# The last 512 output columns of a decoder block: gate folded into the weights, residual seeded into PSUM, result copied out in two halves

## The chip, the cores and the metric

The kernel runs on one NeuronCore of a Trainium2 chip. The metric is the device time of one execution in microseconds (us). The kernel before was timed three times: 1174.56, 1174.75 and 1174.26 us, median 1174.56 us. One further execution was recorded by the hardware profiler; it took 1173.49 us, and 1171.6 us of that lie between its first and its last instruction (its span). All rows of the profile below come from that one execution.

Engines are named as in the profile: PE is TensorE (matmuls; PEld are its weight loads), DVE is VectorE, ACT is ScalarE, POOL is GpSimd, SP is SyncE, which here only issues DMAs.

## What is computed

One decoder block on 256 tokens (t) of 2048 columns, everything in float32:

```
mod = silu(c) @ w_ada + b_ada;  sh1, sc1, g1, sh2, sc2, g2 = split(mod, 6)
h    = rms_norm(x) * (1 + sc1) + sh1
q, k, v, gb, gc, xt = split(h @ w_in, 6)                 # w_in 2048 x 6144
mixed = [rms_norm(attention(q, k, v)), rms_norm(gb * conv(gc * xt))]
x    = x + g1 * (mixed @ w_out)                          # w_out 2048 x 2048
h2   = rms_norm(x) * (1 + sc2) + sh2
u    = conv(h2 @ w_ffn_up)                               # w_ffn_up 2048 x 11264
ffn  = (silu(u_gate) * u_up) @ w_ffn_down                # w_ffn_down 5632 x 2048
out  = x + g2 * ffn
```

The change is about the last line. The 2048 columns of out are four groups of 512, called f = 0 to 3; g2 is one number per column.

## The kernel before

**Products.** Each float32 weight tile ("raw", 128 rows x 1024 columns: two blocks of 512) is split on the chip: ACT writes a rounded copy "hi" (line 947), and DVE or POOL writes "lo" = raw - hi (line 958). The activations are split alike. A product is three matmuls into one PSUM bank: a\*hi, a\*lo and b\*hi (lines 1194 to 1196, a and b being the two parts of the activations), or in the up projection a wide one and a narrow one (lines 1545 and 1549).

**Slots.** All weights, w_in, w_out, w_ffn_up and w_ffn_down, form one list of 205 slots of at most four blocks. While PE multiplies slot i, the program of that step lets ACT, DVE and POOL split slot i+2. SP issues all weight loads in the list's order; a load goes out when one of ten raw buffers comes free, which is when a lo is done. There are six hi and six lo buffers, so a hi waits for PE to be through with an older slot. Which step a piece of side work stands in, whether it goes ahead of or behind the splits, and whether a slot's lo's are made by POOL (table 'pool') is a dictionary of numbers, CFG, written out by hand; an engine executes its instructions in that order.

**The FFN.** The 22 groups of up columns come in four segments of 8, 5, 5 and 4; behind each segment stand the down slots for its rows of w_ffn_down. Sums of the first three segments are kept in SBUF (da). For the last one, `gate_down(f)` (lines 1518 to 1523, two token tiles of 128 each) makes x = x + g2 \* da, with g2 of the 512 columns spread over the partitions in the tile gB. So x then holds the residual and three quarters of the FFN, already gated. The last segment's down slots are 193 to 204, in the order f = 0, 1, 0, 1, 0, 1, 2, 3, 2, 3, 2, 3, with 3, 3 and 2 blocks each. So f = 3 has the slots 200, 202 and 204, and 204 is the last of the kernel; its products are ordered by token tile, all of t = 0 first.

**The end.** When f's last slot is multiplied, `evac_down` does this for each of the two token tiles:

```
y = p * gB                                               # line 1513, DVE, 128x512
y = y + x1                                               # line 1514, DVE, 128x512
out rows <- y                                            # line 1515, DMA of 256 KB, issued by SP
```

Of the kernel before, what the change touches and what calls it, by code (L numbers as in the profile page):

```python
# [234 lines left out]
               108: 3,  # L235
               109: 4,
               159: 2,
               171: 3},
# [56 lines left out]
                72: 0,  # L295
                83: 0},
       'pool_h': [4, 5, 6, 7, 8, 9, 10, 11, 15],
       'psum': [[0, 45]],
# [169 lines left out]
                 'evac_in q1 False': 2,  # L468
                 'evac_in q1 True': 3,
                 'evac_in v0 False': 2,  # L470
# [189 lines left out]
                'up_conv 0': (-1, 0.5),  # L660
                'up_conv 1': (-1, 0.5),
                'up_conv 14': (0, -1),
                'up_conv 15': (0, -0.5),
# [74 lines left out]
       'evac': [5, 0, 1],  # L738
       'sq': [3, 6, 0],
       'tr': [4, 7, 1],  # L740
       'part': -1,
       'up': [[1, 3], [1, 3], [0, 0], [2, 2]],
       'gate': [-21, -14, -2, -11],
       'cls': {'add': 2,
# [34 lines left out]
               'qk_root': 0,  # L779
               'evac_out': 1},  # L780
       'la': 2,
       'h_act': True,
       'h_lag': 1,
       'hi_late': [1, 2, 3, 5, 7, 8, 9, 10, 13, 14, 15, 17, 19, 20, 21, 25, 26, 27, 32, 33, 34, 40, 49, 50, 51, 52, 55, 56,
# [3 lines left out]


@with_exitstack  # L790
def tile_block(
# [74 lines left out]
    nc.vector.memset(ones, 1.0)  # L866
    c32 = const.tile([P, P], F32, name="c32")
    nc.vector.memset(c32, 1.0 / 32.0)
    mask = const.tile([P, 384], F32, name="mask")
    nc.gpsimd.memset(mask, 0.0)  # L870
# [70 lines left out]

    def split_hi(nb):
        ts, his = [], []
        for i in range((nb + 1) // 2):
            m = min(2, nb - 2 * i) * 512
            t = take()
            act(piece(his, "hi")[:, :m], t[:, :m], AF.Copy)  # L947
            ts.append((t, m))
        halfway.append((ts, his))
# [36 lines left out]
    class Ada:  # L986


        def __init__(self, part, c0, n, pe, psum=False):
            self.part, self.c0, self.n, self.pe, self.psum = part, c0, n, pe, psum or pe  # L990
            self.rows = 2048 // n
            self.tiles = NK // self.rows
            self.nch = n // P
            self.w = min(n, 512 if self.psum else n)
            self.seen = 0
            self.out = False
            self.own = [] if [part, c0] in CFG["own"] else None

        def want(self, r):
# [12 lines left out]
        def start(self):  # L1012
# [4 lines left out]
            else:  # L1017
                self.acc = [(t4k if self.n > 512 else t2k)(what)[:, :self.n]]

        def consume(self, r, part=None):  # L1020
            if r == 0 and part != 1:
# [4 lines left out]
            for j in range(self.rows) if part is None else range(8 * part, 8 * part + 8):  # L1026
                i = self.rows * r + j
                x = j * self.n % size
                if x == 0:
                    h = take() if self.own is None else self.own.pop(0)  # L1030
                t, last = h[:, x:x + self.n], self.own is None and x + self.n == 1024
# [45 lines left out]
        def cols(self):  # L1077
# [3 lines left out]
            for a in range(0, self.nch, 4):  # L1081
                m = min(4, self.nch - a)
                p = bank(f"adac{self.part}_{self.c0}", full=False)
                if self.nch == 1:
                    mm(p[:, 0:1], self.chunk(0), ones[:, 0:1], start=True, stop=True)
                    z = p[:, 0:1]
                else:
                    for k in range(m):
                        nc.tensor.transpose(p[:, k * P:(k + 1) * P], self.chunk(a + k), ident)
                    z = bank(f"adaz{self.part}_{self.c0}")[:, :m]  # L1090
                    V.tensor_reduce(out=z, in_=p[:, :m * P].rearrange("p (k q) -> p k q", q=P), axis=AX.X, op=ALU.add)
                self.finish(z, self.c0 + a, m, scale)

        def finish(self, z, c0, m, scale):
# [405 lines left out]
    def evac_down(seg, f):  # L1500
# [31 lines left out]
    for seg, (ga, gb_) in enumerate(SEGS):  # L1532
# [200 lines left out]
    def att_s(h):  # L1733
# [5 lines left out]
        s = t2k("s")[:, :384]  # L1739
        V.tensor_tensor(out=s, in0=p[:, :384], in1=mask, op=ALU.add)  # L1740
        m, z = small(2, "m"), small(2, "z")
        V.reduce_max(out=m[:, 0:1], in_=s[:, :128], axis=AX.X)
        V.reduce_max(out=m[:, 1:2], in_=s[:, 128:], axis=AX.X)
        i, j = (col("q", t, h) for t in range(2))
# [191 lines left out]
    for t in range(2):  # L1936
        xr.append([sb.tile([P, 1024], F32, tag="lo" if t else "hi", bufs=N_HL, name="xr") for _ in range(2)])
        for i in range(2):
            nc.sync.dma_start(xr[t][i], x[0, t * P:(t + 1) * P, i * 1024:(i + 1) * 1024])
    vb, nb = rows("vb", [(by_p(norm1_g[0]), 16), (by_p(b_ada[0]), 96)], nc.sync)  # L1940
    for _ in range(N_RAW):
# [53 lines left out]
    def slot(i):  # L1995
        more = i + LA < len(slots)
        hi_late = i == N_OUT or i in CFG["hi_late"]
        if more and not hi_late:
            split_hi(slots[i + LA][1])
        now[0] = i  # L2000
# [5 lines left out]
        if more and hi_late:  # L2006
            split_hi(slots[i + LA][1])
        steps_of(CFG["pre"].get(i, 1))
# [7 lines left out]
        if i > 1:  # L2016
            slots[i][2](*splits.pop(0))
        for g, r in extra.get(i, []):
            g.consume(r)

# [106 lines left out]
```

## Time and profile before

| | |
|---|---|
| runs of the kernel before | 1174.56, 1174.75, 1174.26 us; median 1174.56 |
| profiled execution | 1173.49 us, its span 1171.6 us |
| PE busy | 1155.4 us (99% of the span), 5989 matmuls |
| DVE, ACT, POOL busy | 917.6 (78%), 646.9 (55%), 169.3 (14%) us |
| POOL's lo's (line 958) | 61, mean 2489 ns; the same shape on DVE 1248 ns |
| clock of TensorE | 0.998 of full speed |
| HBM traffic | 320 MB, 272 GB/s over the span |

How to read it: times in a timeline are us from the span's start. A bracket behind an instruction is how long its engine had idled ahead of it and what ended the idle time. Consecutive like instructions can be put together in one row ("x4"); then the duration is from the first one's start to the last one's end. Neighbouring rows of one engine may overlap by some hundredths, since an engine is pipelined. m('D', 3, 2)0 in the names is the PSUM bank of segment 3, column group f = 2, token tile 0.

### The profile page before, as it was taken

What the parts mean: (1) busy time and instruction counts of PE and PEld (TensorE: products, weight loads), DVE (VectorE), ACT (ScalarE), POOL (GpSimd) and SP (SyncE); (2) the same over time, 40 slices, a digit from 0 to 9 for tenths busy, and PEclk for the clock granted to TensorE, in tenths of its full rate; (3) what the DMA queues carried; (4) which work ended last, traced back from release to release, by engine and by line L of the source; (5) the groups of instructions that cost most, each with busy time, mean ns of one, the idle gap of its engine ahead of it and who ended that gap; (6) DMA issues with size and microseconds to landing.
All of it is one profiled execution on the core that took longest, in us unless ns stands there. A gap on an engine that the chain in (4) does not pass through costs nothing.

```text
span 1171.6 us, 17108 instructions
## 1 busy us (share of the span) xinstructions
PE 1155.4 (99%) x5989; PEld 965.8 (82%) x5989; DVE 917.6 (78%) x1311; ACT 646.9 (55%) x1002; POOL 169.3 (14%) x100
## 2 busy tenths in 40 slices
PE   7999999999999999999999999999999999999998
PEld 5678888878777878888888888888888888888886
DVE  4469979997788989999999544768888897666785
ACT  4666565578566455556676444555435554445461
POOL 0768673631001021000000000000000000000000
PEclk9999999999999999999999999999999999999999
DMA  9999999995799989986465755576887877875541
GB/s 349 405 405 374 406 353 386 390 388 170 262 368 315 362 272 360 378 276 208 156 207 187 235 180 181 175 230 220 284 299 262 306 245 231 292 246 174 169 155 72
DMA packets 205382, 320.22 MB, mean 273 GB/s; under 512 B 13816, under 2 KB 112300, under 8 KB 205296
## 3 DMA queue, kind: packets, MB, share of 16 engines
q1 hardware_dynamic: 202336, 314.68, 77.2%
q10 hardware_dynamic: 2352, 4.22, 1.3%
q8 instruction: 47, 0.77, 0.3%
q14 instruction: 39, 0.32, 0.1%
q0 software_dynamic: 608, 0.23, 0.1%
HBM read 314.87 MB, written 4.21 MB: 272 GB/s over the span
## 4 chain that ended last, share of the span: by engine, by line
PE 91%; DMA 5%; DVE 3%; issue 1%; ACT 0%; POOL 0%; SPq 0%; DVEq 0%; POOLq 0%; ACTq 0%
PE z L1545 27%; PE z L1549 14%; DMA raw<-in_w_in_dram 2%; DMA raw<-in_w_ada_dram 2%; PE ada L1034 1%; PE mx L1194 1%; PE mx L1196 1%; PE mx L1195 1%; PE mk L1194 1%; DVE ada L1051 1%; PE mg L1194 1%; PE mg L1196 1%; PE mc L1194 1%; PE mq L1194 1%; PE mc L1196 1%; PE mg L1195 1%
## 5 line engine op out<-in xcount | busy, mean ns | idle before, releaser
L947 ACT ACTIVATE hi<-raw 128x1024 fp32r<-128x1024 f32 (+1 forms) x401 | 401.2, 1030 | 314.2 <-PE z L1545 92.9
L958 DVE TENSOR_TENSOR lo<-raw,hi 128x1024 fp32r<-128x1024 f32 x340 | 397.6, 1208 | 95.6 <-ACT hi L947 90.3
L1545 PE MATMUL z<-h,hi 128*128 128x512 f32 x1408 | 328.9, 390 | 0.0
L1545 PEld LDWEIGHTS z<-h,hi 128*128 128x128 f32 x1408 | 261.3, 188 | 52.6 <-DVE h L1440 0.3
L1051 DVE SCALAR_TENSOR_TENSOR ada<-raw,csil,ada 128x512 f32<-128x512 f32 (+2 forms) x215 | 189.0, 892 | 5.6 <-DMA raw<-in_w_ada_dram 2.0
L958 POOL TENSOR_TENSOR lo<-raw,hi 128x1024 fp32r<-128x1024 f32 x61 | 150.5, 2489 | 269.2 <-ACT hi L947 269.2
L1549 PEld LDWEIGHTS z<-h,lo 128*128 128x128 f32 x1408 | 174.8, 192 | 3.4
L1549 PE MATMUL z<-h,lo 128*128 128x256 f32 x1408 | 176.0, 283 | 0.0
L1110 POOL MEMSET gb<- 128x512 f32 x2 | 1.1, 526 | 491.8 <-DVE uy L1484 491.8
L1461 DVE TENSOR_TENSOR ub<-z,ub 128x256 f32<-128x256 f32 x120 | 43.8, 417 | 34.5 <-ACT ub L1458 34.4
L1458 ACT ACTIVATE ub<-z 128x256 f32<-128x256 f32 x120 | 39.7, 383 | 31.1 <-PE z L1545 31.0
L1477 ACT ACTIVATE uy<-ub,vcols 128x256 f32<-128x256 f32 x88 | 45.6, 593 | 6.8 <-DMA gr<-gs 6.7
L1482 DVE SCALAR_TENSOR_TENSOR uy<-ub,vcols,uy 128x255 f32<-128x255 f32 x88 | 42.1, 479 | 5.7 <-ACT uy L1477 5.6
L1484 DVE SCALAR_TENSOR_TENSOR uy<-ub,vcols,uy 128x254 f32<-128x254 f32 x88 | 42.5, 483 | 3.1
L1493 ACT ACTIVATE gh<-uy 128x512 fp32r<-128x512 f32 x22 | 13.9, 630 | 40.6 <-DVE uy L1491 40.6
L1487 ACT ACTIVATE uy<-uy 128x512 f32<-128x512 f32 x22 | 13.9, 633 | 37.2 <-DVE uy L1484 37.2
L1034 PE MATMUL ada<-raw,crep 128*32 128x512 f32 (+1 forms) x224 | 27.1, 525 | 3.2 <-DMA raw<-in_w_ada_dram 2.7
L1494 DVE TENSOR_TENSOR gl<-uy,gh 128x512 fp32r<-128x512 f32 x22 | 15.2, 693 | 17.9 <-ACT gh L1493 17.9
L1194 PE MATMUL mk<-hi,h 128*128 128x512 f32 x64 | 25.8, 403 | 0.0
L1194 PE MATMUL mq<-hi,h 128*128 128x512 f32 x64 | 25.3, 395 | 0.4 <-ACT pa_g L1214 0.4
L1194 PE MATMUL mg<-hi,h 128*128 128x512 f32 x64 | 25.7, 401 | 0.0
L1194 PE MATMUL mx<-hi,h 128*128 128x512 f32 x64 | 25.3, 396 | 0.0
(574 smaller groups left out, 1922.8 us busy)
## 6 DMA issues: line engine op xcount, KB each, us to landing
raw<-in_w_ada_dram SPq DMA_DIRECT2D x180, 512.0 KB, 6.8
raw<-in_w_ffn_up_dram SPq DMA_DIRECT2D x352, 256.0 KB, 4.7
raw<-in_w_in_dram SPq DMA_DIRECT2D x95, 512.0 KB, 7.1
raw<-in_w_ffn_down_dram SPq DMA_DIRECT2D x76, 512.0 KB, 4.7
raw<-in_w_out_dram SPq DMA_DIRECT2D x32, 512.0 KB, 6.1
raw<-in_w_ada_dram SPq DMA_DIRECT2D x24, 256.0 KB, 6.6
raw<-in_w_ffn_down_dram SPq DMA_DIRECT2D x24, 256.0 KB, 3.8
xr<-in_x_dram SPq DMA_DIRECT2D x4, 512.0 KB, 5.4
```

Source lines behind the costliest of these rows:

```text
L947: act(piece(his, "hi")[:, :m], t[:, :m], AF.Copy)
L958: (nc.gpsimd if pool in (i + 1, 3) else V).tensor_tensor(out=piece(los, "lo")[:, :m], in0=t[:, :m], in1=hi[:, :m].bitcast(F32), op=ALU.sub ...
L1034: mm(self.acc[0][q:q + 32, :], crep[:, i, :], t, start=(r == 0 and j < 4), stop=(r == self.tiles - 1 and j >= self.rows - 4), tile_positio ...
L1051: V.scalar_tensor_tensor(out=self.acc[n], in0=v, scalar=csil[:, i:i + 1], in1=acc, op0=ALU.mult, op1=ALU.add)
L1194: mm(o, a, hi[k], start=(first and k == 0 and not seeded), stop=False, skip_group_check=True)
L1458: act(c[ft // 2][:, (ft % 2) * 256:(ft % 2) * 256 + 256], zp[grp][ft][:, 256:], AF.Copy)
L1461: V.tensor_tensor(out=d, in0=zp[grp][ft][:, :256], in1=d, op=ALU.add)
L1477: act(y, b, AF.Identity, bias=fcols[3][:, i:i + 1], scale=fcols[2][:, i:i + 1])
L1482: V.scalar_tensor_tensor(out=y[:, 1:], in0=b[:, :255], scalar=fcols[1][:, i:i + 1], in1=y[:, 1:], op0=ALU.mult, op1=ALU.add)
L1484: V.scalar_tensor_tensor(out=y[:, 2:], in0=b[:, :254], scalar=fcols[0][:, i:i + 1], in1=y[:, 2:], op0=ALU.mult, op1=ALU.add)
L1545: mm(zp[grp][ft], blk(hi, j)[:, ft * P:(ft + 1) * P], h2T[k + j], start=k + j == ks[0], stop=k + j == ks[1] - 1)
L1549: mm(zp[grp][ft][:, :256], blk(lo, j)[:, ft * P:(ft + 1) * P], h2T[k + j][:, :256], start=False, stop=False)
```

## The change

For f = 3 of the last segment three things are different, switched by a new entry `'tail': [3]`:

- the raw weights of slots 200, 202 and 204 are multiplied in place by gB on DVE before they are split (line 971 of the changed kernel): three tiles of 128x1024 and two of 128x512. So the products come out gated;
- `seed_down(3)` lets ACT copy x of the two token tiles into the two PSUM banks (now named ms), one step ahead of slot 200, and all products are added onto it;
- `evac_down` only copies out: for each token tile DVE copies the first 256 columns, ACT the last 256, and each half has a DMA of 128 KB of its own, the first issued by SP, the second by ACT.

Beside it the tables are changed. Lo's go from DVE to POOL: both of slot 153, the first of slots 187, 188 and 189, both of slot 200 (in the table 'pool', 1 is the first, 3 both). One subtraction of h goes from POOL to DVE. `gate_down` for f = 2 and 3 comes four and five steps earlier (187 for 191, 177 for 182). At the second norm one DVE step of the ada projection goes from between the two token tiles of z to behind them, ahead of n2m. Some other pieces (a transposition of constants with its copy, squares of the attention output, one residual) come one or two steps earlier or in another order within a step. A constant tile of 128x128 is 128x32. The new entries 'lag', 'sets', 'xq' and 'ttr' are empty or off, and their code makes no instruction.

```diff
+                153: 3,
+                187: 1,
+                188: 1,
+                189: 1,
+                200: 3},
-       'pool_h': [4, 5, 6, 7, 8, 9, 10, 11, 15],
+       'pool_h': [5, 6, 7, 8, 9, 10, 11, 15],
...
-                'evac_c 3 1': (0, 1),
+                'evac_c 3 1': (0, 0.5),
...
-       'gate': [-21, -14, -2, -11],
+       'gate': [-21, -14, -6, -16],
...
+       'tail': [3],
...
-    def split_hi(nb):
+    gated = {}
+
+    def split_hi(n):
+        nb = slots[n][1]
         ts, his = [], []
         for i in range((nb + 1) // 2):
             m = min(2, nb - 2 * i) * 512
             t = take()
+            if n in gated:
+                w = t[:, :m].rearrange("p (k f) -> p k f", f=512)
+                V.tensor_tensor(out=w, in0=w, in1=gB[G2, gated[n]].unsqueeze(1).to_broadcast([P, m // 512, 512]),
+                                op=ALU.mult)
             act(piece(his, "hi")[:, :m], t[:, :m], AF.Copy)
...
             p = mainp["D", seg, f][t]
-            if seg == 0:
+            if seg == len(SEGS) - 1 and f in CFG["tail"]:
+                y = t2k(f"d{f}{t}")
+                V.tensor_copy(y[:, :256], p[:, :256])
+                act(y[:, 256:], p[:, 256:], AF.Copy)
+                for eng, a in ((nc.sync, 0), (nc.scalar, 256)):
+                    eng.dma_start(out[0, t * P:(t + 1) * P, f * 512 + a:f * 512 + a + 256], y[:, a:a + 256])
+            elif seg == 0:
...
+    def seed_down(f):
+        assert f"gd{f}" in done
+        key = "D", len(SEGS) - 1, f
+        whole[key] = None
+        mainp[key] = [bank(f"ms{f}{t}", keep=True, seed=True) for t in range(2)]
+        for t in range(2):
+            act(mainp[key][t], x1[t, f], AF.Copy)
...
+            if seg == len(SEGS) - 1 and f in CFG["tail"]:
+                gated[len(slots)] = f
+                if k == ka:
+                    put(len(slots) - 1, CFG["cls_seed"], seed_down, f)
```

The instructions and waits of three places, before and after. First DVE, whose last twelve instructions ahead of the end are these in the kernel before (d is the tile that goes to the output, x the residual; a wait names the engine or DMA queue):

```order
L958 TENSOR_TENSOR lo<-raw,hi 128x1024 [waits DMAHW4_49,Activation_49]
L958 TENSOR_TENSOR lo<-raw,hi 128x512 [waits DMAHW5_49,Activation_49]
L958 TENSOR_TENSOR lo<-raw,hi 128x1024 [waits DMAHW6_49,Activation_49]
L958 TENSOR_TENSOR lo<-raw,hi 128x1024 [waits DMAHW7_49,Activation_49]
L1513 TENSOR_TENSOR d_11383<-m('D', 3, 2)0_11259,gB_2_9773 128x512 [waits PE_49]
L1514 TENSOR_TENSOR d_11383<-d_11383,x_02_10095 128x512 [waits DVE_49]
L1513 TENSOR_TENSOR d_11387<-m('D', 3, 2)1_11260,gB_2_9773 128x512 [waits PE_49]
L1514 TENSOR_TENSOR d_11387<-d_11387,x_12_10097 128x512 [waits DVE_49]
L1513 TENSOR_TENSOR d_11391<-m('D', 3, 3)0_11295,gB_2_9773 128x512 [waits PE_49]
L1514 TENSOR_TENSOR d_11391<-d_11391,x_03_10131 128x512 [waits DVE_49]
L1513 TENSOR_TENSOR d_11395<-m('D', 3, 3)1_11296,gB_2_9773 128x512 [waits PE_49]
L1514 TENSOR_TENSOR d_11395<-d_11395,x_13_10133 128x512 [waits DVE_49]
```

And these in the changed kernel:

```order
L984 TENSOR_TENSOR lo<-raw,hi 128x1024 [waits Activation_49]
L984 TENSOR_TENSOR lo<-raw,hi 128x512 [waits Activation_49]
L984 TENSOR_TENSOR lo<-raw,hi 128x1024 [waits DMAHW6_49,Activation_49]
L971 TENSOR_TENSOR raw<-raw,gB_2_9773 128x1024 [waits DMAHW7_49]
L984 TENSOR_TENSOR lo<-raw,hi 128x1024 [waits Activation_49]
L1571 TENSOR_TENSOR d_11390<-m('D', 3, 2)0_11265,gB_2_9773 128x512 [waits PE_49]
L1572 TENSOR_TENSOR d_11390<-d_11390,x_02_10095 128x512 [waits DVE_49]
L1571 TENSOR_TENSOR d_11394<-m('D', 3, 2)1_11266,gB_2_9773 128x512 [waits PE_49]
L1572 TENSOR_TENSOR d_11394<-d_11394,x_12_10097 128x512 [waits DVE_49]
L1560 COPY d_11398<-ms_11245 128x256 [waits PE_49]
L1560 COPY d_11403<-ms_11246 128x256 [waits PE_49]
```

The last four instructions of 128x512 have become two copies of 128x256, and a multiplication by gB stands between the lo of slot 203 and the lo of slot 204 (the last lo).

Second ACT. Its last rows in the kernel before, ahead of the end, are the hi's of slots 202, 203 and 204:

```order
L947 ACTIVATE hi<-raw 128x1024 [waits DMAHW4_49,DVE_49,PE_49]
L947 ACTIVATE hi<-raw 128x512 [waits DMAHW5_49,DVE_49,PE_49]
L947 ACTIVATE hi<-raw 128x1024 [waits DMAHW6_49,DVE_49,PE_49]
L947 ACTIVATE hi<-raw 128x1024 [waits DMAHW7_49,DVE_49,PE_49]
L2122 UNCONDITIONAL_BRANCH
```

In the changed kernel, from the seeds on:

```order
L1589 ACTIVATE ms_11245<-x_03_10131 128x512
L1589 ACTIVATE ms_11246<-x_13_10133 128x512
L973 ACTIVATE hi<-raw 128x1024 [waits DMAHW2_49,PE_49,Activation_49]
L973 ACTIVATE hi<-raw 128x512 [waits DMAHW3_49,PE_49,Activation_49]
L973 ACTIVATE hi<-raw 128x1024 [waits DVE_49,PE_49,Activation_49]
L973 ACTIVATE hi<-raw 128x512 [waits DVE_49,PE_49,Activation_49]
L973 ACTIVATE hi<-raw 128x1024 [waits DMAHW6_49,PE_49,Pool_49]
L973 ACTIVATE hi<-raw 128x1024 [waits DVE_49,PE_49,Pool_49]
L1561 ACTIVATE d_11398<-ms_11245 128x256 [waits DVE_49]
L1563 DMA out_dram<-d_11398 128x256 [waits Activation_49]
L1561 ACTIVATE d_11403<-ms_11246 128x256 [waits DVE_49]
L1563 DMA out_dram<-d_11403 128x256 [waits DMAHW1_49,Activation_49]
```

ACT's half of each token tile waits for DVE, not for PE, and its DMA stands behind it on ACT's own queue; the hi's of the gated slots wait for DVE's multiplication.

Third POOL, from its last MEMSET but one on, before:

```order
L1110 MEMSET gb_2622 128x512
L1112 DMA gb_2622<-in_b_ada_dram 1x16x32 x4
L958 TENSOR_TENSOR lo<-raw,hi 128x1024 x7
L1110 MEMSET gb_9752 128x512
L1112 DMA gb_9752<-in_b_ada_dram 1x16x32 x4
L2122 UNCONDITIONAL_BRANCH
```

And in the changed kernel:

```order
L1162 MEMSET gb_2622 128x512
L1164 DMA gb_2622<-in_b_ada_dram 1x16x32 x4
L984 TENSOR_TENSOR lo<-raw,hi 128x1024 x9
L1162 MEMSET gb_9752 128x512
L1164 DMA gb_9752<-in_b_ada_dram 1x16x32 x4
L984 TENSOR_TENSOR lo<-raw,hi 128x1024 x4
L984 TENSOR_TENSOR lo<-raw,hi 128x512
L2229 UNCONDITIONAL_BRANCH
```

Two lo's more stand ahead of the last MEMSET (slot 153's), and five behind it, where POOL had none (those of slots 187 to 189 and of slot 200).

More of the change, by code (lines that the diff above doesn't have):

```diff
@@ L236 @@
                109: 4,
+               148: 2,
                159: 2,
@@ L738 @@
        'evac': [5, 0, 1],
-       'sq': [3, 6, 0],
+       'sq': [3, 4, 0],
        'tr': [4, 7, 1],
@@ L779 @@
                'qk_root': 0,
-               'evac_out': 1},
+               'evac_out': 1,
+               'cols_set': -1},
        'la': 2,
@@ L784 @@
        'hi_late': [1, 2, 3, 5, 7, 8, 9, 10, 13, 14, 15, 17, 19, 20, 21, 25, 26, 27, 32, 33, 34, 40, 49, 50, 51, 52, 55, 56,
[3 rows of a table removed]
[3 rows of a table added]
+       'tail': [3],
+       'lag': {},
+       'sets': [],
+       'xq': False,
+       'ttr': False}
 @with_exitstack
@@ L866, in tile_block @@
     nc.vector.memset(ones, 1.0)
-    c32 = const.tile([P, P], F32, name="c32")
+    c32 = const.tile([P, 32], F32, name="c32")
     nc.vector.memset(c32, 1.0 / 32.0)
+    pick = {}
+    for v in (1.0, 1.0 / 32.0):
+        if CFG["sets"]:
+            pick[v] = const.tile([P, 39], F32, name=f"pick{int(1 / v)}")
+            nc.gpsimd.memset(pick[v], 0.0)
+            nc.gpsimd.memset(pick[v][:, 7:8], v)
     mask = const.tile([P, 384], F32, name="mask")
@@ L997, in __init__ @@
             self.own = [] if [part, c0] in CFG["own"] else None
+            self.held = {}
         def want(self, r):
@@ L1018, in start, with hold @@
                 self.acc = [(t4k if self.n > 512 else t2k)(what)[:, :self.n]]
+        def hold(self, r):
+            tiles = self.rows * self.n // (1024 if self.own is None else 512)
+            self.held[r] = [take() if self.own is None else self.own.pop(0) for _ in range(tiles)]
         def consume(self, r, part=None):
@@ L1029, in consume @@
                 if x == 0:
-                    h = take() if self.own is None else self.own.pop(0)
+                    src = self.held.get(r, self.own)
+                    h = take() if src is None else src.pop(0)
                 t, last = h[:, x:x + self.n], self.own is None and x + self.n == 1024
@@ L1092, in cols, with cols_set @@
                 self.finish(z, self.c0 + a, m, scale)
+        def cols_set(self):
+            groups = self.set
+            p = bank(f"adas{self.part}_{self.c0}", full=False)
+            parts = [(g, a) for g in groups for a in range(0, g.nch, 4)]
+            for n, (g, a) in enumerate(parts):
+                assert g.out
+                flush(g)
+                e = pick[1.0 / 32.0 if g.pe else 1.0][:, 7 - n:39 - n]
+                m = min(4, g.nch - a)
+                for q in range(m):
+                    mm(p[32 * q:32 * q + 32, :P], e, g.chunk(a + q), start=n == 0, stop=n == len(parts) - 1,
+                       tile_position=(0, 32 * q))
+            r = t1k("adar")[:, :P]
+            act(r, p[:, :P], AF.Copy)
+            p = bank(f"adat{self.part}_{self.c0}", full=False)
+            nc.tensor.transpose(p[:, :P], r, ident)
+            for n, (g, a) in enumerate(parts):
+                m = min(4, g.nch - a)
+                g.finish(p[:, n:n + 32 * m - 31:32], g.c0 + a, m, 1.0)
         def finish(self, z, c0, m, scale):
@@ L1598, in tile_block, with in_set @@
     ready_at = {}
+    held_until = {}
+    sets = {(part, c0): n for n, e in enumerate(CFG["sets"]) for part, c0 in e}
+    filling = {}
+    def in_set(g, s):
+        n = sets.get((g.part, g.c0))
+        if n is None:
+            return False
+        filling.setdefault(n, []).append((s, g))
+        if len(filling[n]) < len(CFG["sets"][n]):
+            return True
+        s, gs = max(s for s, _ in filling[n]), [g for _, g in filling[n]]
+        gs[0].set = gs
+        at(s + 2, gs[0].cols_set)
+        ready_at.update({(g.part, g.c0 + k): s + 2 for g in gs for k in range(g.nch)})
+        return True
     def spread_loads(g, a, span):
@@ L1604, in spread_loads @@
             extra.setdefault(s, []).append((g, r))
+            lag = CFG["lag"].get(f"{g.part} {g.c0}", 0)
+            if lag:
+                s += lag
+                held_until.setdefault(s, []).append((g, r))
         at(s + 1, g.evac)
+        if in_set(g, s):
+            return
         if g.gate():
@@ L1647, in tile_block @@
             at(a, g.evac)
+            if in_set(g, a - 1):
+                continue
             at(a + 1, g.cols)
@@ L1739, in att_s @@
         s = t2k("s")[:, :384]
-        V.tensor_tensor(out=s, in0=p[:, :384], in1=mask, op=ALU.add)
         m, z = small(2, "m"), small(2, "z")
-        V.reduce_max(out=m[:, 0:1], in_=s[:, :128], axis=AX.X)
-        V.reduce_max(out=m[:, 1:2], in_=s[:, 128:], axis=AX.X)
+        if CFG["ttr"]:
+            for t, a, b in ((0, 0, 128), (1, 128, 384)):
+                V.tensor_tensor_reduce(out=s[:, a:b], in0=p[:, a:b], in1=mask[:, a:b], scale=1.0, scalar=NEG,
+                                       op0=ALU.add, op1=ALU.max, accum_out=m[:, t:t + 1])
+        else:
+            V.tensor_tensor(out=s, in0=p[:, :384], in1=mask, op=ALU.add)
+            V.reduce_max(out=m[:, 0:1], in_=s[:, :128], axis=AX.X)
+            V.reduce_max(out=m[:, 1:2], in_=s[:, 128:], axis=AX.X)
         i, j = (col("q", t, h) for t in range(2))
@@ L1938, in tile_block @@
         for i in range(2):
-            nc.sync.dma_start(xr[t][i], x[0, t * P:(t + 1) * P, i * 1024:(i + 1) * 1024])
-    vb, nb = rows("vb", [(by_p(norm1_g[0]), 16), (by_p(b_ada[0]), 96)], nc.sync)
+            (nc.scalar if CFG["xq"] and t else nc.sync).dma_start(
+                xr[t][i], x[0, t * P:(t + 1) * P, i * 1024:(i + 1) * 1024])
+    vb, nb = rows("vb", [(by_p(norm1_g[0]), 16), (by_p(b_ada[0]), 96)], nc.gpsimd if CFG["xq"] else nc.sync)
     for _ in range(N_RAW):
@@ L1998, in slot @@
         if more and not hi_late:
-            split_hi(slots[i + LA][1])
+            split_hi(i + LA)
         now[0] = i
@@ L2006, in slot @@
         if more and hi_late:
-            split_hi(slots[i + LA][1])
+            split_hi(i + LA)
         steps_of(CFG["pre"].get(i, 1))
@@ L2018, in slot @@
         for g, r in extra.get(i, []):
+            if f"{g.part} {g.c0}" in CFG["lag"] and (g, r) not in fill:
+                g.hold(r)
+            else:
+                g.consume(r)
+        for g, r in held_until.get(i, []):
             g.consume(r)
```

9 lines of the change are left out of this document (5 added, 4 removed), and 6 rows, old and new, of tables.

## Prediction

> **What bounds the kernel now.** I read the page's busy times first, then busy time by stretches, then PE's waits, and last the chain that ends the kernel. The page and the stretches:
>
> ```profile
> PE 1155.4 (99%) x5989; PEld 965.8 (82%) x5989; DVE 917.6 (78%) x1311; ACT 646.9 (55%) x1002; POOL 169.3 (14%) x100
> 0.00:41.00 41.00, 31.65 (x212) 20.74 (x213) 18.24 (x45) 19.93 (x33) 7.67 (x12) 0.96 1.00 362
> 41.00:440.00 399.00, 396.76 (x1906) 316.04 (x1905) 330.16 (x504) 245.86 (x425) 156.15 (x83) 1.00 0.94 346
> 440.00:800.00 360.00, 360.00 (x1970) 314.15 (x1969) 284.30 (x395) 203.96 (x303) 2.98 (x1) 1.00 0.70 230
> 800.00:1162.00 362.00, 362.00 (x1886) 311.04 (x1885) 279.52 (x362) 177.18 (x242) 2.49 (x5) 1.00 0.69 231
> ```
>
> The columns after the length are the busy times of PE, PEld, DVE, ACT and POOL, then the granted clock, the share of the DMA engines and GB/s. From 440 to 1162 us PE is busy for 360.00 of 360.00 and 362.00 of 362.00 us, at full clock. Nothing that another engine does there can make the kernel faster; it can only make PE wait. From 41 to 440 us PE loses 2.2 us, and its waits name these:
>
> ```profile
> PE n2b L1414 <- DVE n2d L1412: 1.0, 1, 1.0
> PE as L1737 <- ACT kT L1730: 0.9, 1, 0.9
> PE mq L1194 <- ACT pa_g L1214: 0.4, 1, 0.4
> ```
>
> Ahead of 41 us PE loses 9.35 us while the DMA engines are at 1.00; in that stretch only the constant tile is smaller. So the change can gain at two places: in those 2.3 us of waits, and behind the last products. The end, by the chain of waits, PE's last matmul and SP:
>
> ```profile
> 1162.97 0.70 DVE d L1513
> ...
> 1167.78 0.69 DVE d L1514
> 1166.62 0.39 PE L1196 MATMUL m('D', 3, 3)1_11296<-hi,gl 128*128 128x512 f32 x1
> 1168.50 0.33 SPq L1515 DMA_DIRECT2D out_dram<-d  x1
> DMA to landing us min/median/max: 2.3/2.3/2.3
> ```
>
> The chain runs through eight DVE instructions from 1162.97 on, and one could think that halving DVE's work brings 2.7 us. It does not. PE's last matmul ends at 1166.62 + 0.39 = 1167.01, and by its timeline DVE starts on that bank at 1167.05:
>
> ```profile
> 1167.05 0.69 DVE L1513 TENSOR_TENSOR d<-m('D', 3, 3)1_11296,gB 128x512 f32<-128x512 f32 x1
> ```
>
> So DVE was ready just as the products were. Behind PE's end lie 0.04 us of hand-over, two instructions until 1168.47, 0.03 us until SP issues, 2.3 us until landing (1170.8), and 0.8 us until the span's end at 1171.6. Only the first part, 1.46 us from 1167.01 to 1168.47, can shrink.
>
> **The change part by part: the end.** The bank is now copied out in two halves. Neither a DVE copy of 128x256 out of PSUM nor an ACT copy of exactly this kind is in the trace. The nearest rows:
>
> ```profile
> L880 DVE COPY vbc<-pv_vbc x1: 268/268/268, 12.8 to 12.8; 128x112 f32<-128x112 f32 x1
> L1986 DVE COPY vcols<-pv_f x1: 586/586/586, 143.1 to 143.1; 128x418 f32<-128x418 f32 x1
> L1458 ACT ACTIVATE ub<-z 128x256 f32<-128x256 f32 x120 | 39.7, 383 | 31.1 <-PE z L1545 31.0
> L1203 ACT ACTIVATE mg<-pa_g 128x512 f32<-128x512 f32 x8 | 4.5, 585 | 0.1
> ```
>
> DVE: (586 - 268) / (418 - 112) = 1.04 ns a column, so 268 + 144 x 1.04 = 0.42 us; bounds 0.27 and 0.59. ACT: 0.38 us, a read of 128x256 out of PSUM; no less, and at most the 0.59 of twice the columns. The words of the change suggest that both run side by side. The order of instructions says otherwise: ACT's half waits for DVE, and for nothing of PE's. So they run one after the other: 1167.05 + 0.42 = 1167.47 for DVE, 0.04 of hand-over (as from PE to DVE), 0.38 on ACT, end at 1167.89. ACT issues its DMA 0.03 later, at 1167.92, where SP issued at 1168.50. **Gain 0.58 us.** SP's half goes out at 1167.50 and is not last. With the bounds of the two copies the gain is 0.73 to 0.21 us.
>
> The landing. No transfer of 128 KB into HBM is in the trace; all eight of out, 256 KB from SP, land in 2.3 us. From ACT's queue there are:
>
> ```profile
> gB<-gr ACTq DMA_DIRECT2D x8, 256.0 KB, 3.1
> pk<-x ACTq DMA_DIRECT2D x8, 256.0 KB, 4.5
> 1168.83:1170.81 1.98, 0.00 (x0) 0.00 (x0) 0.00 (x0) 0.00 (x0) 0.00 (x0) 0.87 0.34 132
> ```
>
> I take 2.3, since the other two ran beside weight loads and the end has nothing beside it. Upper bounds are 3.1 and 4.5: 0.8 and 2.2 us more. Downwards: during the last landing the DMA engines are busy for 0.34 x 1.98 = 0.67 us, and half the bytes can save half of that, 0.34 us. [...]
>
> **Gating.** DVE gets three multiplications of 128x1024 and two of 128x512 with two inputs in SBUF, priced as a lo, 1248 ns, and as the 0.69 us of line 1514 above:
>
> ```profile
> L958 DVE TENSOR_TENSOR lo<-raw,hi 128x1024 fp32r<-128x1024 f32 x316 | 383.0, 1248 | 91.3 <-ACT hi L947 85.9 <-PE z L1549 3.0 <-DMA raw<-in_w_ffn_down_dram 0.8
> 1149.22 1.82 DVE L958 TENSOR_TENSOR lo<-raw,hi 128x1024 fp32r<-128x1024 f32 x2
> 1157.56 0.39 PE L1195 MATMUL m('D', 3, 3)0_11295<-lo,gh 128*128 128x512 f32 x1
> 1153.18 2.59 DVE L958 TENSOR_TENSOR lo<-raw,hi 128x1024 fp32r<-128x1024 f32 x2 [2.14 <-ACT hi L947]
> 1162.97 0.69 DVE L1513 TENSOR_TENSOR d<-m('D', 3, 2)0_11259,gB 128x512 f32<-128x512 f32 x1 [7.20 <-PE m('D', 3, 2)0_11259 L1196]
> 1164.36 0.39 PE L1195 MATMUL m('D', 3, 3)0_11295<-lo,gh 128*128 128x512 f32 x1
> ```
>
> That is 3 x 1.25 + 2 x 0.69 = 5.1 us more, and for slot 200 two lo's (1.9 us) fewer. It is hidden: slot 202's first lo is made from 1149.22 to 1150.44, and PE wants it at 1157.56, 7.1 us later; slot 204's lo ends at 1153.18 + 2.59 = 1155.77, and PE wants it at 1164.36. In slot 204 the chain gets longer by one multiplication and, since hi now follows it behind slot 203's lo, one hi (1.06): 1155.8 + 1.2 + 1.1 = 1158.1, 6 us early. DVE's 7.20 us of idle time after it take it up; without that cover each 128x1024 would cost its 1.25 us. The seeds are two ACT copies of 0.59 us, while ACT idles between its hi's:
>
> ```profile
> 1142.62 1.06 ACT L947 ACTIVATE hi<-raw 128x1024 fp32r<-128x1024 f32 x1 [2.09 <-PE m('D', 3, 0)1_11099 L1196]
> ```
>
> They lie ahead of this row, in the 2.09 us of idle time that it shows, and nothing is queued behind them but the hi of slot 201. Taken at nothing; uncovered 1.2 us.
>
> **The tables.** Seven lo's go to POOL, where one takes 2489 ns for DVE's 1248. The tightest is the first of slot 188:
>
> ```profile
> 1087.08 2.00 ACT L947 ACTIVATE hi<-raw 128x1024 fp32r<-128x1024 f32 x2
> 1093.62 4.00 PE L1549 MATMUL z<-h,lo 128*128 128x256 f32 x32
> L958 POOL TENSOR_TENSOR lo<-raw,hi 128x1024 fp32r<-128x1024 f32 x61 | 150.5, 2489 | 269.2 <-ACT hi L947 269.2
> ```
>
> Its hi is done at 1088.1, so POOL at 1090.6; PE wants it in the second half of this row, from 1095.5 on: 4.9 us to spare. The raw buffer comes free 1.2 us later, and SP's next load with it; its hi's have idle time as above. All at nothing. The second norm's wait (n2b) hangs on ACT, which is why I take the moved ada step at nothing too:
>
> ```profile
> 426.97 0.75 DVE L1051 SCALAR_TENSOR_TENSOR ada<-raw,csil,ada 128x512 f32<-128x512 f32 x1
> 428.56 0.63 ACT L1406 ACTIVATE x1s<-x 128x512 f32<-128x512 f32 x1
> 429.17 0.63 ACT L1406 ACTIVATE x1s<-x 128x512 f32<-128x512 f32 x1
> 429.92 0.16 DVE L1407 SCALAR_TENSOR_TENSOR n2m<-n2q,ss 128x2 f32<-128x2 f32 x1 [0.82 <-ACT x1s L1406]
> ```
>
> ACT's two squares follow one another, so x being ready 0.75 us earlier does not start the second earlier; the ada step then fits into DVE's 0.82 us of idle time. The earlier `gate_down` moves four DVE instructions of 0.69 us within stretches without any PE wait.
>
> **The sum.** Span 1171.6 - 0.58 = 1171.0 us; with the 1.9 us around it 1172.9 us for the profiled execution. That one lies 1.07 us below the median of the runs, so the median goes from 1174.56 to **1174.0 us**. A difference under 0.2% (2.35 us) counts as no change here.
>
> **Rivals.**
> (A) The end gains more. If ACT's half does not really lose time on DVE's, the later of the two ends at 1167.47, 1.0 us earlier than before; with 0.34 us off the landing 1.34. That gives 1173.2 to 1173.6. For it: half the bytes. Against it: the wait in ACT's queue.
> (B) The waits in the middle close too: 1.0, 0.9 and 0.4 us. All three with the 0.58 give 1171.7, the norm's alone 1173.0. For it: the tables are changed right there (ada step, order of pieces near q). Against it: the ACT rows above for the largest, and a step that is moved rarely closes a wait without opening another.
> (C) The last half lands later because it comes from ACT's queue in rows of 1 KB: 3.1 or 4.5 us for 2.3, so 0.2 or 1.6 us slower than before in the span, 1174.8 to 1176.2. Against it: no other traffic at the end.
> (D) Slower: POOL's new lo's are held up by DVE. That the two get in each other's way is in the trace:
>
> ```profile
> 420.17 2.41 POOL L958 TENSOR_TENSOR lo<-raw,hi 128x1024 fp32r<-128x1024 f32 x1 [2.66 <-ACT hi L947]
> 420.72 2.41 DVE L1301 TENSOR_TENSOR x<-y,x 128x512 f32<-128x512 f32 x1
> ```
>
> An addition of this shape takes DVE 0.69 us at the end (line 1514 above) and took 2.41 beside POOL's lo, 3.5 times as long. If POOL lost by the same factor, 8.7 us for a lo, slot 188's would be done at 1088.1 + 8.7 = 1096.8, 1.3 us late. In slot 200 POOL starts at about 1140.8: DVE's lo's ahead end at 1135.51 + 2.96 = 1138.47 (the first row below), the gate takes 1.25 and hi 1.06. Then 8.7, and half of that for the second piece of 128x512, end at 1153.9, where PE wants it at 1152.12: 1.7 us late.
>
> ```profile
> 1135.51 2.96 DVE L958 TENSOR_TENSOR lo<-raw,hi 128x1024 fp32r<-128x1024 f32 x3 [0.26 <-DMA raw<-in_w_ffn_down_dram]
> 1152.12 0.39 PE L1195 MATMUL m('D', 3, 3)0_11295<-lo,gh 128*128 128x512 f32 x1
> ```
>
> Together 3.0 - 0.58 = 2.4 us: the median at 1177.0, or later with slot 153's pair. It decides from three times 2489 ns on. [...] Against it: it was DVE that lost here, while POOL took 2.41 us, and POOL's mean over 61 lo's is 2489, most of them beside a busy DVE. If DVE is the one that loses, it is by some 1.7 us at a time against 5 us and more of slack.
>
> **How the numbers follow.** Forecast 0.62, its own range 1173.6 to 1174.6 (gain of 0.21 to 0.73 with 0.25 us for the runs' spread). A 0.12, B 0.09, C 0.10, D 0.07. A range from 1172.4 to 1176.0 leaves out D, most of B and the end of C, about 0.16. Faster by over 0.2%, below 1172.2, needs nearly all of B: 0.06. Slower by over 0.2%, above 1176.9, is D and a remainder: 0.08. Same: 0.86.
>
> **What would show it.** Right: ACT's half in the last bank starts after DVE's copy has ended, near 1167.5; its DMA is issued near 1167.9; the last landing takes 2.3 us; PE has no wait between 440 us and its end, which stays near 1167.0; span near 1171.0. Wrong: both halves starting together (A); n2b's wait gone (B); a last landing of 3 us or more (C); PE waiting for POOL's lo in slots 153, 188 or 200, or POOL's lo's far above 2.5 us (D). A PE end that moves by more than 1 us would make the sum wrong at its root.

## The result, and the profile after

The changed kernel takes **1181.61 us** (median of five runs, 1180.88 to 1183.19), the kernel before 1174.56: a ratio of 1.0065 with a 95% interval of 1.0052 to 1.0079. So it is slower, by 7 us, where 0.6 us less had been forecast. Its profiled execution took 1180.98 us with a span of 1179.2 us, 7.6 us more than before.

Busy time by stretches, columns as in the prediction (length, PE, PEld, DVE, ACT, POOL, clock, DMA share, GB/s), changed kernel:

```profile
0.00:41.00 41.00, 30.51 (x204) 19.88 (x204) 17.85 (x44) 19.91 (x33) 5.93 (x11) 1.00 1.01 342
41.00:440.00 399.00, 393.58 (x1866) 311.96 (x1865) 324.79 (x488) 239.82 (x414) 156.10 (x83) 1.00 0.95 340
440.00:800.00 360.00, 359.97 (x1967) 312.79 (x1967) 283.22 (x402) 203.18 (x303) 2.98 (x1) 1.00 0.72 234
800.00:1162.00 362.00, 362.00 (x1901) 311.69 (x1900) 289.45 (x367) 182.79 (x254) 19.89 (x12) 1.00 0.72 236
```

Behind 440 us PE is as full as before, with the gating, the seeds and POOL's new lo's (19.89 for 2.49 us of POOL between 800 and 1162) among it. All that was lost was lost ahead of it. There the DMA engines are as busy as they were (1.01 and 0.95), but move less: 342 for 362 GB/s, 340 for 346. PE's five longest waits behind the start-up now:

```profile
PE mg L1246 <- ACT mg L1255: 1.9, 1, 1.9
PE n2b L1466 <- DVE n2d L1464: 1.0, 1, 1.0
PE as L1833 <- DVE adae L1083: 0.8, 1, 0.8
PE mv L1246 <- ACT pa_k L1266: 0.8, 1, 0.8
PE mk L1246 <- ACT pa_v L1266: 0.6, 1, 0.6
```

The waits for mg, mv and mk are new. In ACT's timeline the first of them goes back to a weight load. ACT seeds mg behind the hi's of a w_in slot, and these waited for their weights:

```profile
153.81 1.06 ACT L973 ACTIVATE hi<-raw 128x1024 fp32r<-128x1024 f32 x1 [4.34 <-DMA raw<-in_w_in_dram]
156.12 1.10 ACT L1255 ACTIVATE mg<-pa_g 128x512 f32<-128x512 f32 x2
```

The same products of mg on PE, before and, in the second fence, in the changed kernel:

```profile
150.42 0.50 PE L1194 MATMUL mg<-hi,h 128*128 128x512 f32 x1
152.82 0.39 PE L1195 MATMUL mg<-lo,h 128*128 128x512 f32 x1
```

```profile
156.76 0.50 PE L1246 MATMUL mg<-hi,h 128*128 128x512 f32 x1 [1.93 <-ACT mg L1255]
160.49 0.63 PE L1247 MATMUL mg<-lo,h 128*128 128x512 f32 x1
157.50:161.00 3.50, 3.50 (x10) 2.68 (x10) 3.24 (x5) 1.53 (x2) 2.64 (x2) 0.52 1.06 392
```

PE is 6.34 us late at the first of them and 7.67 at the second, ten matmuls later: behind the wait of 1.93 us the granted clock was 0.52 for some 3.5 us. At the end of the program it is 8.05 us late (PE's last product ends at 1175.06 for 1167.01). So nearly all of the loss lies ahead of 160 us, where loads set the pace.

The rate of the loads shows it directly. GB/s in 40 equal slices of the first 41 us, before:

```profile
GB/s 0 40 162 266 420 396 272 336 368 384 385 384 387 385 384 384 384 384 384 431 406 426 394 418 424 376 384 385 383 384 413 420 420 377 383 392 405 383 386 394
```

And in the changed kernel:

```profile
GB/s 0 60 227 256 408 388 264 342 384 366 351 349 348 347 349 349 349 347 349 368 387 391 406 398 412 393 376 358 349 348 349 358 384 408 380 358 357 359 370 364
```

The plateau of 384 has become one of 349, in a stretch where the order of instructions and loads is the same. In the stretches from 0 to 41, 41 to 130 and 130 to 250 us the loads moved 342, 381 and 377 GB/s for 362, 396 and 383 before, so 2.9 MB less by 250 us; at 380 GB/s that is an estimated 7.6 us, about what was lost. What is not the same is an address. The constant tile c32 is 128x32 instead of 128x128, 384 bytes a partition shorter, and all tiles laid out behind it start 384 bytes earlier: by the memory layout of the compiled programs the first raw buffer is at byte 76928 of each partition instead of 77312. 77312 is a multiple of 256; 76928 is 128 past one.

The end of the kernel did nearly what was forecast. DVE and ACT rows of the last bank, the issue, and the landings of all DMAs into out:

```profile
1175.10 0.42 DVE L1560 COPY d<-ms 128x256 f32<-128x256 f32 x1 [0.94 <-PE ms L1248]
1175.56 0.38 ACT L1561 ACTIVATE d<-ms 128x256 f32<-128x256 f32 x1 [0.97 <-DVE d L1560]
1175.97 0.34 ACTq L1563 DMA_DIRECT2D out_dram<-d  x1
DMA to landing us min/median/max: 1.9/2.3/2.3
```

From PE's end to the last issue it is 0.91 us for 1.49: the 0.58 of the prediction. From that issue to the end of the span it is 3.23 for 3.10. So 4.14 us lie behind PE's end instead of 4.59, 0.45 less. The landing of 1.9 us is that of ACT's last half, the last issue of all.

### The profile page after: what moved, and what is told of

Same layout as the page of the kernel before. It is cut to its first block, busy times and chain, and to the rows that moved or that the text cites. A ratio compares the mean times of both kernels' runs of the same rounds, so it can differ in the third digit from the quotient of the medians.

```text
span 1179.2 us, 17121 instructions
## 1 busy us (share of the span) xinstructions
PE 1159.1 (98%) x5989; PEld 966.8 (82%) x5989; DVE 921.8 (78%) x1308; ACT 647.5 (55%) x1006; POOL 184.9 (16%) x106
## 4 chain that ended last, share of the span: by engine, by line
PE 86%; DVE 6%; DMA 6%; issue 1%; ACT 1%; SPq 0%; DVEq 0%; ACTq 0%
PE z L1611 27%; PE z L1615 14%; DMA raw<-in_w_ada_dram 3%; DVE ada L1083 3%; DMA raw<-in_w_in_dram 2%; PE ada L1066 1%; PE mg L1246 1%; PE mg L1247 1%; PE mg L1248 1%; DVE lo L984 1%; PE mx L1246 1%; PE mx L1248 1%; PE mx L1247 1%; PE mc L1248 1%; PE mc L1247 1%
## 5 line engine op out<-in xcount | busy, mean ns | idle before, releaser
L984 DVE TENSOR_TENSOR lo<-raw,hi 128x1024 fp32r<-128x1024 f32 (+1 forms) x333 | 392.2, 1216 | 98.9 <-ACT hi L973 93.4
L1611 PE MATMUL z<-h,hi 128*128 128x512 f32 x1408 | 328.9, 390 | 0.0
L984 POOL TENSOR_TENSOR lo<-raw,hi 128x1024 fp32r<-128x1024 f32 x68 | 166.8, 2475 | 923.6 <-ACT hi L973 923.5
L1083 DVE SCALAR_TENSOR_TENSOR ada<-raw,csil,ada 128x512 f32<-128x512 f32 (+2 forms) x215 | 193.0, 911 | 7.1 <-DMA raw<-in_w_ada_dram 3.5
L1123 DVE TENSOR_REDUCE adaz<-adac 128x4 f32<-128x512 f32 (+1 forms) x18 | 11.4, 635 | 21.4 <-PE adac L1121 21.4
L1246 PE MATMUL mv<-hi,h 128*128 128x512 f32 x64 | 25.3, 396 | 0.8 <-ACT pa_k L1266 0.8
L1247 PE MATMUL mg<-lo,h 128*128 128x512 f32 x64 | 25.7, 401 | 0.0
```

What stands on the lines that cost most here:

```text
L984: (nc.gpsimd if pool in (i + 1, 3) else V).tensor_tensor(out=piece(los, "lo")[:, :m], in0=t[:, :m], in1=hi[:, :m].bitcast(F32), op=ALU.sub ...
L1083: V.scalar_tensor_tensor(out=self.acc[n], in0=v, scalar=csil[:, i:i + 1], in1=acc, op0=ALU.mult, op1=ALU.add)
L1246: mm(o, a, hi[k], start=(first and k == 0 and not seeded), stop=False, skip_group_check=True)
L1247: mm(o, a, lo[k], start=False, stop=False, skip_group_check=True)
L1611: mm(zp[grp][ft], blk(hi, j)[:, ft * P:(ft + 1) * P], h2T[k + j], start=k + j == ks[0], stop=k + j == ks[1] - 1)
```

## The experiments

Theory A: the addresses slow the loads. Its rival T: the moved table entries make w_in's stage wait. Later rival E: it is where the engines' operands lie. All kernels were timed beside the kernel before, whose medians in the three rounds were 1173.97, 1173.61 and 1174.02 us. Two of its 61 executions there took 1180.75 and 1181.22 us, the others at most 1176.79, so a single execution proves little. The ratio with its interval is the one on record and can differ by some 0.1% from the quotient of the medians. The changed kernel is "after", and "raw", "hi, lo" and "512 tiles" are the offsets of these buffers from a multiple of 512 bytes (the last are the 128x512 tiles, which hold the activations h, gh, gl and a few early loads).

| kernel | raw | hi, lo | 512 tiles | us | ratio, interval |
|---|---|---|---|---|---|
| after | 128 | 128 | 128 | 1181.61 | 1.0065, 1.0052 to 1.0079 |
| after, c32 wide | 0 | 0 | 0 | 1174.97 | 1.0004, 0.9995 to 1.0013 |
| before, c32 128x32 | 128 | 128 | 128 | 1183.30 | 1.0066, 1.0047 to 1.0085 |
| raw and 512 tiles shifted | 128 | 0 | 128 | 1197.64 | 1.0197, 1.0179 to 1.0215 |
| hi, lo at 128, rest at 256 | 256 | 128 | 256 | 1191.53 | 1.0145, 1.0129 to 1.0160 |
| raw alone | 128 | 0 | 0 | 1179.35 | 1.0050, 1.0035 to 1.0065 |
| all but raw | 0 | 128 | 128 | 1175.59 | 1.0008, 0.9988 to 1.0027 |
| all by 256 bytes | 256 | 256 | 256 | 1173.47 | 1.0004, 0.9995 to 1.0013 |
| all by 64 bytes | 448 | 448 | 448 | 1180.87 | 1.0067, 1.0050 to 1.0085 |
| 512 tiles alone | 0 | 0 | 128 | 1193.25 | 1.0159, 1.0145 to 1.0172 |

**The constant undone and done alone.** On the changed kernel, and the other way round on the kernel before:

```diff
-    c32 = const.tile([P, 32], F32, name="c32")
+    c32 = const.tile([P, P], F32, name="c32")
```

> The changed kernel with the constant tile c32 at 128x128 again, nothing else undone. In the changed kernel that tile is 384 bytes a partition shorter, and every tile that is laid out behind it (the raw, hi and lo buffers, the 128x512 and smaller ones) starts 384 bytes earlier: at 128 past a multiple of 256 bytes, where it was at a multiple before. Theory A (addresses): loads into such buffers are slower, 349 for 384 GB/s in the steady stretch of the start, and the weight-bound stage up to 250 us takes the 8 us from it. Then this run is at 1174.0 us, the time of the prediction, with PE's last product near 1167.0. Theory T (tables): the pieces of work that were put earlier around 134 to 160 us (constants transposed a slot earlier, another order near q) make PE wait for w_in. Then it stays near 1181.6.

> The kernel before with that one constant tile at 128x32 and nothing else of the change. Theory A: 1181.5 us or a little more (1174.5 + the 8 us that PE lost, less nothing at the end: 1182). Theory T: no change, 1174.5.

1174.97 and 1183.30 us; in the first the plateau is at 384 GB/s again, in the second at 349. The one line accounts for the loss from both sides, and T falls as its cause: with all tables of the changed kernel and the wide constant there is no difference that this measurement can tell. Both came out about 1 us above what A expected. With the wide constant 4.14 us lie behind PE's end, as in the changed kernel, but PE ends at 1167.76 instead of 1167.01, so the gain at the end isn't seen in the time.

**Where the shift counts, first attempt.** Pads in front of and behind the raw buffers, in the kernel before:

```diff
+    pad0 = sb.tile([P, 32], F32, tag="pad0", bufs=1, name="pad0")
+    nc.gpsimd.memset(pad0, 0.0)
     for _ in range(N_RAW):
         load_next()
```

(the first of the two runs has a second such pad behind the loop, the other has the constant at 128x32).

> The kernel before, with a pad of 128 bytes a partition ahead of the raw buffers and one of 128 bytes further behind, so that the raw buffers and the 128x512 tiles start at 128 past a multiple of 256 bytes, while constants, hi, lo and the small tiles lie at multiples of 256 as before. Theory A, if it is where the DMAs write that counts: 1181 to 1182. If it is rather the operands of the engines (hi, lo): 1174.5. Theory T: 1174.5.

> The kernel before with the constant at 128x32 and a pad of 128 bytes ahead of the raw buffers: hi and lo start at 128 past a multiple of 256 bytes, the raw buffers and what lies behind them at a multiple of 256 again, though not of 512. Theory A, if where the DMAs write counts and 256 bytes are the grain: 1174.5. If the grain is 512 bytes, or if the engines' operands count: 1178 to 1182. Theory T: 1174.5.

1197.64 and 1191.53 us: far more than either theory had, so they don't decide about A. The start was at 349 GB/s in the first and at 384 in the second, as A says. But PE itself had become slower, all the way to the end. The wide product of the up projection in the second of these runs:

```profile
L1545 PE MATMUL z<-h,hi 128*128 128x512 f32 x1408 | 336.5, 395 | 0.0
```

Before and in the changed kernel the same row has 328.9, 390. In both runs with pads hi and the 512 tiles, the two operands of a matmul, lie at different offsets; in the changed kernel they are shifted alike.

**Second attempt.** A second pad (behind the first load, which lays out all ten raw buffers) brings the rest back to its place, so that hi and the 512 tiles keep the same offset:

```diff
+    pad0 = sb.tile([P, 32], F32, tag="pad0", bufs=1, name="pad0")
+    nc.gpsimd.memset(pad0, 0.0)
+    load_next()
+    pad1 = sb.tile([P, 96], F32, tag="pad1", bufs=1, name="pad1")
+    nc.gpsimd.memset(pad1, 0.0)
-    for _ in range(N_RAW):
+    for _ in range(N_RAW - 1):
         load_next()
```

(and the mirror image, constant at 128x32, pads of 96 and 32 columns).

> The kernel before; the ten raw buffers alone start at 128 past a multiple of 256 bytes, hi, lo, the 128x512 and the smaller tiles at multiples of 512 as before (pads of 128 and 384 bytes around the raw buffers). Theory A, now as: what counts is where the weight loads write. Then the steady rate of the start is 349 GB/s for 384, and the time 1181 to 1184 as with the narrow constant. Rival E: it is where the engines' operands lie (hi, lo, 128x512): 1174. In both, matmuls of 512 columns follow one another every 226.7 ns; in the two runs with pads before it was 233 ns, and I put that down to hi and the 128x512 tiles, the two operands of a matmul, starting at different places modulo 256 bytes, which they do not here. If the pads as such (one memset more) did that, it is 233 here too and the time 1190 and more.

> The mirror image: the kernel before with everything behind the constant at 128 past a multiple of 256 bytes, as in the changed kernel, but the ten raw buffers at multiples of 512. Theory A: 1174 to 1175 (a few early loads go to 128x512 tiles, which lie off), start at 384 GB/s. Rival E: 1181 to 1184. Matmuls every 226.7 ns in both, since both operands of a matmul are shifted alike.

1179.35 and 1175.59 us. GB/s between 14 and 25 us, raw alone shifted:

```profile
GB/s 350 339 346 376 372 380 384 380 387 384 387 384 380 384 380 387 384 391 376 380 398 421 410 451 402 425 387 410 425 410 425 454 417 372 387 417 387 410 410 439
```

All but raw shifted:

```profile
GB/s 387 384 380 387 387 380 380 384 384 384 354 346 350 350 343 343 354 358 343 350 346 365 380 391 428 402 380 417 417 417 425 417 484 372 350 395 425 439 380 402
```

The two kernels change places within this stretch. The first loads go to raw buffers: 350 where these are shifted, 384 where they are not. The loads behind them go to 512 tiles, and the rates are exchanged. (The rate of 349 therefore did not hold through the whole start, as had been expected for raw alone.) So it is the place where a load writes that counts; E falls as the main cause. The time of raw alone is under the 1181 to 1184 that A expected; 2.6 us of its loss had built up at mg's first product (152.98 us), and behind it PE waited 2.0 us for mv and 2.2 us for as. Matmuls followed one another as before in both (wide rows at 390 ns), so the pads as such did not slow PE. Whether the 2 us of the second kernel are more than its early loads into 512 tiles can't be told: its interval holds no difference.

**The grain.** Constant tile at 128x64 and at 128x112, in the kernel before:

> The kernel before with the constant tile at 128x64: everything behind it starts 256 bytes earlier, at 256 past a multiple of 512. Theory A with a grain of 256 bytes or less: 1174, 384 GB/s at the start. With a grain of 512: 1181 to 1184, 349 GB/s.

> The kernel before with the constant tile at 128x112: everything behind it starts 64 bytes earlier, at 192 past a multiple of 256. Theory A with a grain of 128 or 256 bytes: 1181 to 1184 as with 128 bytes off. If only the grain of 64 counted, the run with the narrow constant would not have been slow, so 1174 here would contradict A.

1173.47 and 1180.87 us: 256 bytes cost nothing, 64 bytes as much as 128 as far as can be told. GB/s in 40 slices of the first 41 us, 256 bytes off and, in the second fence, 64 bytes off:

```profile
GB/s 0 40 179 288 424 340 272 316 374 387 385 386 384 386 384 384 384 384 386 440 390 446 376 432 404 386 387 382 383 385 411 415 424 375 383 391 409 383 383 395
```

```profile
GB/s 0 32 182 262 440 348 292 344 365 352 350 350 349 348 347 349 349 349 348 347 393 396 428 362 414 412 374 361 349 347 351 346 379 413 391 363 350 356 375 363
```

The plateaus are 384 and 349. So the grain, the step whose multiples cost nothing, is 256 bytes for these loads in rows of 1 KB: smaller ones are excluded by the changed kernel, which is 128 off, larger ones by the first of these two. The price is the same at 64 and at 128 bytes off, 349 / 384 = 0.91 of the rate. Only the written side was moved; why it has this grain, no run shows.

**The end, alone.** The changed code with all tables and the constant of the kernel before; and the same with each bank copied out whole:

```diff
-                V.tensor_copy(y[:, :256], p[:, :256])
-                act(y[:, 256:], p[:, 256:], AF.Copy)
-                for eng, a in ((nc.sync, 0), (nc.scalar, 256)):
-                    eng.dma_start(out[0, t * P:(t + 1) * P, f * 512 + a:f * 512 + a + 256], y[:, a:a + 256])
+                V.tensor_copy(y, p)
+                nc.sync.dma_start(out[0, t * P:(t + 1) * P, f * 512:(f + 1) * 512], y)
```

> The change at the end alone: gate folded into the weights of f = 3, residual seeded, two halves; all tables of the order and the constant tile as in the kernel before. In the changed kernel 0.91 us lay between PE's end and the last DMA issue, for 1.49 before, and 3.23 from that issue to the end of the span, for 3.10. So 4.14 for 4.59 us behind PE's end: 0.45 us less, 1173.2 where the kernel before has 1173.7. If gating delays a lo (rival D's place without POOL), PE shows waits behind 1140 us and the gain is gone.

> As the tail alone, but each bank copied out whole by DVE and sent by one DMA of 256 KB on SP, instead of a half by DVE, a half by ACT and two DMAs. If the halves run one after the other (0.42 + 0.38 us and two hand-overs), a whole copy of about 0.68 us is shorter: 0.04 + 0.68 + 0.03 = 0.75 us from PE's end to the issue for 0.91, then 3.10: 3.85 us in all, 0.3 less than with halves. If the halves gained by running beside each other it would be longer than 0.91.

With halves: 1173.32 us, ratio 0.9997 (0.9987 to 1.0007); behind PE's end 0.91 us to the issue and 3.19 to the end. With whole copies: 1173.07 us, ratio **0.9988 (0.9980 to 0.9997)**, the one version here whose interval lies below the kernel before, if by 1 us only; it overlaps that of the halves. Its last bank:

```profile
1166.96 0.39 PE L1240 MATMUL ms<-hi,gl 128*128 128x512 f32 x1
1167.38 0.69 DVE L1552 COPY d<-ms 128x512 f32<-128x512 f32 x1 [0.67 <-PE ms L1240]
1168.10 0.33 SPq L1553 DMA_DIRECT2D out_dram<-d  x1
```

From 1167.35 to 1168.10 are 0.75 us, and the span ends at 1171.2: 3.85 us as expected, 0.25 to 0.3 less than with halves. One copy of 0.69 is shorter than 0.42 and 0.38 in a row. The times of the two versions don't separate them; the traces do. PE waited for nothing behind 440 us in this run.

**The tables, alone.**

```diff
-       'tail': [3],
+       'tail': [],
```

(changed kernel, constant wide).

> The changed kernel with the entry 'tail' empty and the constant tile at 128x128: the moved table entries alone, end as before. Theory A: 1174 to 1175, as the run with the wide constant, and 4.59 us behind PE's end. If the tables cost something of their own (waits of PE for mg and as around 150 and 255 us), 0.5 to 1 us above the kernel before.

1175.20 us, ratio 1.0008 (1.0000 to 1.0017): about 1 us slower than the kernel before, at the edge of what can be told. In this profile and in that of the wide constant PE waits 1.2 and 1.1 us for mg, which it does not in the kernel before. But the profile of the tail alone, with the old tables, has that wait too (an execution of 1178.73 us, the longest of its twelve), so which entry does it, if one does, stays open.

**The matmul's two operands.** One pad of 128 bytes, behind the raw buffers only:

> The kernel before with a pad of 128 bytes a partition behind the raw buffers: raw, hi and lo stay at multiples of 512, the 128x512 and smaller tiles (h, gh, gl: the weights side of the matmuls as PE loads them) start at 128 past. Theory P: PE is slower when the two operands of a matmul start at different places modulo 256 bytes, 233.3 for 226.7 ns from one matmul of 512 columns to the next as in the two runs with pads: 16 to 20 us more, 1190 to 1194, with the start still near 384 GB/s. If it was something else in those runs: 1174.

1193.25 us, ratio 1.0159. The first 41 us ran at 349 GB/s in the mean, as in the mirror image (350), for 362 in the kernel before. PE's rows of 32 wide products, in this kernel:

```profile
1081.07 7.63 PE L1545 MATMUL z<-h,hi 128*128 128x512 f32 x32
```

and in the kernel before:

```profile
1086.34 7.44 PE L1545 MATMUL z<-h,hi 128*128 128x512 f32 x32
```

2.6% more for each, at full clock (1.00), though nothing waits: this accounts for the first two runs with pads (19 us here, 18 and 24 there, the latter with shifted loads as well). It has no part in the changed kernel, whose operands moved together (7.44 us there too).

## Why the prediction was wrong

**The step that failed** is the sentence "in that stretch only the constant tile is smaller", from which it went on to two places where the change could gain and none where it could lose ahead of 41 us. The smaller tile was seen and taken at nothing, without a reason. Its price was in the layout: every tile behind it moved by 384 bytes, off the 256-byte grain, and the loads with rows of 1 KB became 9% slower (349 for 384 GB/s), the first 41 us as a whole 6% (342 for 362). The views had shown where that must hurt: DMA engines at 1.00 and 0.94 ahead of 440 us. None of the four rivals had this mechanism, nor did the range reach 1181.6. The prediction's own last sign of being wrong came true: PE's end moved by 8.05 us, where 1 us would have shown the sum to be wrong at its root. With the constant at its old width the median is 1174.97, within the stated range; but that is 1.0 above the kernel before of its round, not 0.6 below, and its interval holds no difference, so the forecast gain isn't shown by it either.

**The terms of the sum** held up to the last issue. DVE's half took 0.42 us, ACT's 0.38, one behind the other as the order of instructions said; the issue came 0.58 us earlier against PE's end. What follows the issue was mis-sized: the last half landed 1.9 us after its issue where 2.3 had been taken (0.34 less was the prediction's lower bound), but from there to the end of the span it was 1.3 us instead of 0.8. So the sooner landing brought nothing, and 0.45 us were left; what fills the 1.3 us isn't shown. **Gating, seeds, POOL's lo's:** PE's last wait is that of the second norm, now at 439 us; behind it there is none, as forecast. POOL's lo's of the full shape in the changed kernel:

```profile
L984 POOL TENSOR_TENSOR lo<-raw,hi 128x1024 fp32r<-128x1024 f32 x67 | 165.2, 2486 | 923.6 <-ACT hi L973 923.5
```

They take 2486 ns in the mean for 2489 before, with seven more of them, six of this shape: rival D did not happen. **The second norm** kept its 1.0 us for n2b, so the ada step was worth nothing there, as said. **Rival A** is excluded by the rows of the last bank, **C** by the landing times. **B** failed: in the changed kernel the wait for mq is gone and the one for as is 0.8, but others came in their place, and with the wide constant all three are there (n2b 1.0, as 1.0, mq 0.3).

Against the 7 us in time, the constant alone makes 6.6 (1181.61 to 1174.97) to 9.3 (1183.30 to 1173.97) by medians, 7.2 to 7.8 by the ratios. Within it not all is slower loading: in the profile of the changed kernel 6.3 us had built up at mg's first product, and 1.3 came in the stretch of low clock behind its wait.

## What to carry to other kernels

A constant's size is also the address of everything behind it: before pricing a smaller or larger tile as one instruction, compare the layout of the two programs, and look whether buffers that loads write into keep their place modulo 256 bytes (off it 349 GB/s for 384 here) and matmul operands theirs to each other (7.63 us for 7.44 here). Where a stage runs at the limit of its loads, a few per cent of their rate go into the time: here 2.9 MB that were missing by 250 us, and 8 us. And where two engines share one bank, read from the order whether they run side by side; here one whole copy reached the end of the span 0.25 to 0.3 us sooner than two halves.

## What the runs showed that was not expected

- Loads into tiles that start off a multiple of 256 bytes ran at 349 GB/s for 384 in rows of 1 KB; 64 and 128 bytes off cost the same as far as can be told (349 both), 256 nothing (384).
- Matmuls whose two operands started at different offsets (128 bytes apart modulo 256) took 7.63 us for 32 products of 512 columns instead of 7.44, and the kernel 19 us more. Why is open; only differences of 128 were tried.
- In the changed kernel a wait of PE of 1.9 us was followed by 3.5 us at a granted clock of 0.52, which cost another 1.3 us; the stretch from 130 to 250 us with this wait is at 0.99 in the mean. In the kernel before with the narrow constant the stretches from 130 to 250 us (a wait of 1.9 us) and from 250 to 440 us (2.2) are at 0.99, in the tail alone that from 250 to 440 us (2.2) is. But with the shift of 64 bytes (1.9), with raw alone shifted (2.0) and with raw and 512 tiles shifted (2.2) the stretches with these waits are at 1.00. So the length of a wait doesn't decide it alone, and what does stays open. Where the waits of such a stretch are all of 1.6 us or less, it is at 1.00.
